# Corner and meta tiles of the first layer turned through VectorE and GpSimd's transfers instead of TensorE, the last heads' splits in another order, and one more group with widened products

## The chip, the cores and the metric

The kernel runs on one core of a Trainium2 chip. The metric is device microseconds of one execution. Three runs of the kernel before took 2268.68, 2270.69 and 2272.91 us (median 2270.69). TensorE does the matrix products, VectorE, ScalarE and GpSimd the work beside them, and the queues of SyncE, ScalarE and GpSimd issue transfers between HBM and the core's memory.

## What is computed

A decoder of two layers on 272 tokens (16 learned meta tokens ahead of 256), width 2048, 16 heads of 128. Layer 0 is attention with forget gates, layer 1 stick-breaking attention with its own keys and values; each is followed by a squared-ReLU MLP of width 8192.

```python
def forgetting_attention(q, k, v, cum_logf):
    for qs, qe in query_blocks(q.shape[1]):      # (0,16), (16,144), (144,272)
        s = jnp.einsum('bqhd,bkhd->bhqk', q[:, qs:qe], k[:, :qe]) * scale
        s = s + cum_logf[:, :, qs:qe, None] - cum_logf[:, :, None, :qe]
        s = jnp.where(mask, s, -jnp.inf)
        p = jax.nn.softmax(s, axis=-1)
        outs.append(jnp.einsum('bhqk,bkhd->bqhd', p, v[:, :qe]))
...
def squared_relu_mlp(h, w_up, w_down):
    u = h @ w_up
    return jnp.square(jax.nn.relu(u)) @ w_down
```

## The kernel before

Activations lie feature-major: 128 features on the partitions, tokens along the row. Every large product is done by `gemm_group`, one call for 512 output columns over all 2048 inputs. Weights and activations are split into a high and a low part (`whi`, `wlo` by L210 on ScalarE and L211 on VectorE; `sp.hi`, `sp.lo`), and each pair gives three products, so a call has 192 products, all issued by L177: 4 blocks `kb` of 4 chunks `kc`, 4 output tiles `m`, 3 parts. In the blocks 0 and 3 the products go output tile by output tile. The calls are counted by `u`: in layer 0 each of four **head groups** g (4 heads) has u = 3g+1 (queries), 3g+2 (keys) and 3g+3 (values); u = 61 to 64 is the output projection of layer 1, u = 89 to 92 the last quarter of its MLP's up projection, u = 93 to 95 the down projection behind it. While the split weights of one block are in use, those of the next are made; `whi`, `wlo` and the raw weights have four buffers each.

In layer 0 a product has 272 columns, from u = 61 on 256. There some products take 6 columns more (L243 to L254, `wide`): they read zeros behind the tile and write columns that nobody uses. Before the change that is done at three places of every fourth call (u % 4 == 1, output tile 3), and at three places of u = 90 (output tile 0), which follows eight products (`ph`, L785) that turn a part of the residual.

Beside the products of the next call runs the attention of a head group. In layer 0, with `s` the probabilities of 4 heads, queries on the partitions:

- `turn_probabilities` and `probabilities_back` (L446 to L459) turn the bulk of the probabilities without TensorE: VectorE turns blocks of 32 by 32 (L451), GpSimd's queue writes them to a scratch in HBM (L454, `p_dram`) and reads them back in the right order (L459). `squares`, `scratch`, `values_back` (L386 to L415) do the same for the values through `v_dram` (L394, L401, L406).
- What is left over are small pieces: the **corners** (`corners`, L434: 16 queries of the one block and 16 of the other, `sm`, or 16 values each, `vc`) and the **meta** values (`packed`, `vm`). TensorE turns them as products with a unit matrix: `pm` (L558) and `pvm` (L572, L573). ScalarE copies `pvm` into `vm_sb` (L575), VectorE makes `pm_sb` from `pm` (L560).
- `pom` (L577, L578) multiplies them, and its two halves go to the result (`put_split`) and to `own` (L581).
- `outputs` (L587), called behind the next call's 192 products, forms `po` (L596, L597) from the turned values and probabilities, adds `own` (L599), and splits the result.

Head group 3 has its values turned by TensorE (`token_major`, L374) as well, in both layers, since no call follows that would cover the transfers.

Nothing of this order on the engines is written out by hand: a scheduler with a simulated timeline places the instructions of each engine. `behind` and `placed_behind` add an order without a wait: the instruction is placed behind another, named by its place in the list `issued` of the current call's products. Each engine and each queue works off its own list in order.

Of the kernel before, what the change touches and what calls it, by code (L numbers as in the profile page):

```python
# [33 lines left out]
def yoco_kernel(ctx: ExitStack, tc: tile.TileContext, hT_in, gains, b_f, w_f, w_qkv0, w_o0, w_up, w_dn,  # L34
                w_kv, w_q1, w_o1, g_row, out):
    nc = tc.nc
# [25 lines left out]
    ident = const.tile([P, P], F32, name="ident")  # L62
# [152 lines left out]
    def gemm_group(wblk, sp, t0, evac, before={}, after={}, load_x=None):  # L215

        uid[0] += 1
        u = uid[0]  # L220
        accs = [pacc.tile([P, 512], F32, tag="acc", name=f"acc_{u}_{m}") for m in range(4)]
        n = T - t0
        for kb in range(4):
            if kb in before:
                before[kb]()
            parts, on_act, on_dve = weights(u, kb, wblk, 16 if t0 else 0, load_x)
            if kb in after:
                with tc.issue_after(on_act.ins), tc.issue_after(on_dve.ins):
                    after[kb]()

            if load_x is not None and kb == 0:
                runs = [([kc], range(4)) for kc in range(4)]
            elif kb in (0, 3):
                runs = [(range(4), [m]) for m in range(4)]
            else:
                runs = [(range(2 * hf, 2 * hf + 2), range(4)) for hf in range(2)]
            pinned[0] = load_x is None
            for kcs, ms in runs:
                pairs = ((0, sp.hi), (0, sp.lo), (1, sp.hi))
                if t0:  # L240
# [133 lines left out]
    def token_major(vT, pr, t0, label):  # L374

        pv = patt.tile([P, 2, 2, P], F32, tag="patt", name=f"pv_{label}")
        for i in range(2):
            for b in range(2):
                nc.tensor.transpose(pv[:, i, b, :], vT[:, 2 * pr + i, t0 + b * P:t0 + b * P + P], ident)
        v0 = att.tile([P, 2, 2, P], F32R, tag="v_sb", name=f"v0_{label}")  # L380
        v1 = tmp.tile([P, T], F32, tag="u2", name=f"v1_{label}")[:, :2 * P].rearrange("p (i d) -> p i d", i=2)
        split(v0, pv[:, :, 0, :])
        nc.scalar.copy(v1, pv[:, :, 1, :])
        return v0, v1

    def squares(vT, tag, label):  # L386

# [84 lines left out]
    for g in range(4):  # L472
# [74 lines left out]
        for pr in range(2):  # L547
# [10 lines left out]
        nc.tensor.transpose(pm[:, 0:P], sm, ident)  # L558
        pm_sb = att.tile([P, 192], F32, tag="pm_sb", bufs=1, name=f"pm_sb_{g}")
        nc.vector.tensor_tensor(out=pm_sb[:, :P].rearrange("p (b q) -> p b q", q=M), in1=maskD, op=ALU.mult,  # L560
                                in0=pm[:, P - M:P].unsqueeze(1).to_broadcast([P, 8, M]))

        gemm_group(w_qkv0[3 * g + 2], xa, 0, lambda m, acc: evac_kv(m, acc, vT))

# [10 lines left out]
        nc.scalar.copy(vm_sb, pv[:, :2 * P])  # L575
        po = patt.tile([P, 512], F32, tag="patt", name=f"pom_{g}")
        nc.tensor.matmul(po[:, :64], vm_sb[:, :P], s0T.rearrange("p (h q) -> p h q", h=4)[:, :, :M], start=True, stop=True)  # L577
        nc.tensor.matmul(po[:, 64:192], vm_sb[:, P:], pm_sb[:, :P], start=True, stop=True)  # L578
        put_split(ao, 4 * g, 4, 0, M, po[:, :64].rearrange("p (h q) -> p h q", h=4))
        own = att.tile([P, 8, M], F32, tag="own", bufs=1, name=f"own0_{g}")  # L580
        copied = nc.scalar.copy(own, po[:, 64:192].rearrange("p (c q) -> p c q", c=8))  # L581
        for pr in range(2):
            behind(split_probabilities(*pps[pr]), issued[-1] if pr == 0 else copied.ins)

        turned = squares(vT, "s", f"0_{g}") if g < 3 else None

        def outputs(g=g, pps=pps, vT=vT, own=own, turned=turned):  # L587
            if turned is not None:
                scratch(turned, issued[20:60:20])
                vs = values_back(turned, issued[100:120:10], issued[160:180:10], f"0_{g}")  # L590
            for pr in range(2):
                p0, p1 = in_order(*pps[pr])
                v0, v1 = vs[pr] if turned is not None else token_major(vT, pr, 0, f"0_{g}_{pr}")
# [100 lines left out]
    for g in range(4):  # L694
# [49 lines left out]
            scratch(turned, issued[-2:])  # L744

        def outputs1(g=g, vT=vT, pps=pps, pm_sb=pm_sb, turned=turned):
            for pr in range(2):
# [4 lines left out]
            nc.tensor.transpose(pv[:, :P], corners(vT[:, :, P:144], vT[:, :, 256:T], f"vc1_{g}"), ident)  # L752
            vc_sb = att.tile([P, P], F32, tag="vm_sb", bufs=1, name=f"vc_sb_{g}")
            nc.scalar.copy(vc_sb, pv[:, :P])
            own = att.tile([P, 8, M], F32, tag="own", bufs=1, name=f"own1_{g}")
            for pr in range(2):
                v0, v1 = vs[pr] if turned is not None else token_major(vT, pr, 0, f"1_{g}_{pr}")
# [152 lines left out]
```

## Time and profile before

| | |
|---|---|
| profiled execution, its own time | 2272.29 us |
| its span, first to last instruction | 2270.6 us |
| three other runs | 2268.68, 2270.69, 2272.91 us |
| TensorE busy | 2261.9 us, 18826 products |
| VectorE, ScalarE, GpSimd busy | 1345.2, 1060.1, 89.9 us |
| mean DMA rate | 190 GB/s |

Busy time says how much of the span an engine had an instruction under way; TensorE's products overlap each other, so what one costs is read from the distance between starts, not from its duration. In the rows of the timeline a row is `start, us, engine, line, operation, out<-in, xcount`, and the bracket at its end is the time that the engine sat idle before it and what ended that. Buffer numbers are left out of names.

### The profile page before, as it was taken

The page shows a single profiled execution, that of the slowest core. Times are in us where ns is not written, and L with a number is a line of the kernel's source. Part 1 is how long each engine was busy: PE and PEld are TensorE (multiplying, and loading weights), DVE is VectorE, ACT ScalarE, POOL GpSimd, SP SyncE. Part 2 cuts the span into 40 slices and gives each one's busy share as a digit, 9 for nine tenths or more (in the row PEclk, how much of TensorE's full clock was granted, in tenths as well). Part 3 has the DMA queues.
Part 4 walks back from the last instruction along what each step waited for, and adds up shares of the span by engine and source line. Part 5 has one row for each costly group of instructions (what it writes and reads, how often), then busy time and mean ns, then how long its engine had stood idle before and what let it go on. Part 6 is the DMA issues. An engine that isn't in the chain of part 4 may idle for free.

```text
span 2270.6 us, 44920 instructions
## 1 busy us (share of the span) xinstructions
PE 2261.9 (100%) x18826; PEld 2254.3 (99%) x18826; DVE 1345.2 (59%) x1947; ACT 1060.1 (47%) x1447; POOL 89.9 (4%) x178
## 2 busy tenths in 40 slices
PE   9999999999999999999999999999999999999998
PEld 9999999999999999999999999999999999999998
DVE  7767666554455455455566677666555555555555
ACT  6444445443354344344444455555444543544544
POOL 1220110000000000000000011100000000000001
PEclk9999999999999999999999999999999999999999
DMA  7765655555555555555555566665656656666564
GB/s 240 232 200 187 220 185 176 182 172 180 183 177 179 175 178 185 176 179 175 176 188 189 179 217 211 212 197 185 202 189 191 202 185 203 189 194 201 180 195 140
DMA packets 126715, 431.47 MB, mean 190 GB/s; under 512 B 15776, under 2 KB 22320, under 8 KB 126512
## 3 DMA queue, kind: packets, MB, share of 16 engines
q1 hardware_dynamic: 119520, 412.59, 56.7%
q0 software_dynamic: 4672, 12.59, 1.8%
q8 instruction: 147, 2.41, 0.4%
q10 hardware_dynamic: 2320, 3.43, 0.4%
q14 instruction: 56, 0.46, 0.1%
HBM read 416.99 MB, written 11.55 MB: 189 GB/s over the span
## 4 chain that ended last, share of the span: by engine, by line
PE 98%; DMA 1%; DVE 0%; issue 0%; ACT 0%; SPq 0%; POOL 0%; POOLq 0%; ACTq 0%
PE acc L177 96%; PE po L420 1%; PE ps L420 0%; PE pz L420 0%; DMA raw<-w_qkv 0%; PE pz L716 0%; PE ps L518 0%; DMA p_dram<-raw_p 0%; DMA raw_p<-p_dram 0%; PE po L597 0%; PE po L765 0%; DVE wlo L211 0%; ACT whi L210 0%; PE pf L339 0%; DVE raw_p L451 0%
## 5 line engine op out<-in xcount | busy, mean ns | idle before, releaser
L211 DVE TENSOR_TENSOR wlo<-raw,whi 128x1024 fp32r<-128x1024 f32 (+1 forms) x773 | 928.2, 1216 | 701.8 <-ACT whi L210 695.3
L210 ACT ACTIVATE whi<-raw 128x1024 fp32r<-128x1024 f32 (+1 forms) x773 | 797.2, 1051 | 973.8 <-PE acc L177 923.4
L177 PE MATMUL acc<-x_m,whi 128*128 128x272 f32 (+1 forms) x4096 | 644.7, 282 | 0.0
L177 PE MATMUL acc<-x_u,whi 128*128 128x272 f32 (+1 forms) x3968 | 626.1, 281 | 0.0
L177 PEld LDWEIGHTS acc<-x_m,whi 128*128 128x128 f32 x4096 | 567.3, 188 | 0.1
L177 PEld LDWEIGHTS acc<-x_u,whi 128*128 128x128 f32 x3968 | 550.3, 188 | 0.0
L177 PE MATMUL acc<-x_m,wlo 128*128 128x272 f32 (+1 forms) x2048 | 441.6, 282 | 0.0
L177 PE MATMUL acc<-x_u,wlo 128*128 128x272 f32 (+1 forms) x1984 | 431.5, 281 | 0.0
L177 PE MATMUL acc<-x_a,whi 128*128 128x272 f32 (+1 forms) x2048 | 353.3, 285 | 0.3 <-ACT whi L210 0.3
L177 PEld LDWEIGHTS acc<-x_m,wlo 128*128 128x128 f32 x2048 | 324.0, 188 | 0.0
L177 PEld LDWEIGHTS acc<-x_u,wlo 128*128 128x128 f32 x1984 | 315.1, 188 | 0.0
L177 PEld LDWEIGHTS acc<-x_a,whi 128*128 128x128 f32 x2048 | 300.7, 188 | 1.6 <-ACT whi L210 1.0
L177 PE MATMUL acc<-x_a,wlo 128*128 128x272 f32 (+1 forms) x1024 | 253.3, 285 | 0.0
L177 PE MATMUL acc<-x_kv,whi 128*128 128x272 f32 x1024 | 192.8, 288 | 0.0
L177 PEld LDWEIGHTS acc<-x_a,wlo 128*128 128x128 f32 x1024 | 175.5, 188 | 0.7 <-DVE ssq_a L143 0.4
L177 PE MATMUL acc<-x_o,whi 128*128 128x272 f32 (+1 forms) x1024 | 162.7, 282 | 0.0
L177 PEld LDWEIGHTS acc<-x_kv,whi 128*128 128x128 f32 x1024 | 160.3, 188 | 0.0
L177 PE MATMUL acc<-x_kv,wlo 128*128 128x272 f32 x512 | 147.4, 288 | 0.0
L177 PEld LDWEIGHTS acc<-x_o,whi 128*128 128x128 f32 x1024 | 141.9, 188 | 0.0
L292 DVE TENSOR_TENSOR hT<-acc,hT 128x272 f32<-128x272 f32 (+1 forms) x156 | 67.4, 432 | 75.4 <-PE acc L177 75.2
L177 PE MATMUL acc<-x_o,wlo 128*128 128x272 f32 (+1 forms) x512 | 110.5, 282 | 0.0
L177 PEld LDWEIGHTS acc<-x_kv,wlo 128*128 128x128 f32 x512 | 96.5, 188 | 0.0
(222 smaller groups left out, 1096.3 us busy)
## 6 DMA issues: line engine op xcount, KB each, us to landing
raw<-w_up SPq DMA_DIRECT2D x256, 512.0 KB, 4.3
raw<-w_dn SPq DMA_DIRECT2D x256, 512.0 KB, 4.4
raw<-w_qkv SPq DMA_DIRECT2D x92, 512.0 KB, 4.2
raw<-w_o SPq DMA_DIRECT2D x64, 512.0 KB, 4.4
raw<-w_kv SPq DMA_DIRECT2D x64, 512.0 KB, 4.5
raw<-w_q SPq DMA_DIRECT2D x32, 512.0 KB, 5.1
p_dram<-raw_p POOLq DMA_DIRECT2D x32, 96.0 KB, 3.7
raw_p<-p_dram POOLq DMA_DIRECT2D x8, 384.0 KB, 5.5
```

The costliest lines, as they stand in the source:

```text
L177: ins = nc.tensor.matmul(*args, **kw).ins
L210: on_act = nc.scalar.activation(hp, src, AF.Copy)
L211: on_dve = nc.vector.tensor_tensor(out=lp, in0=src, in1=hp.bitcast(F32), op=ALU.subtract)
L292: nc.vector.tensor_tensor(out=hT[:, c, t0:], in0=acc, in1=hT[:, c, t0:], op=ALU.add)
L420: product = nc.tensor.matmul(out, a[i], b[j], start=start and k == 0, stop=stop and k == 2)
```

## The change

Three parts, each in words and then in the diff.

**Corners and meta tiles of layer 0.** `corner_turned` (new) turns the corner `sm` on VectorE, 32 partitions by 128, and sends it through a scratch `c_dram` on GpSimd's queue, one write and one read; the result is `pmq`, and VectorE makes `pm_sb` from it. `rows_turned` (new) does so for `vm` and `vc` in head groups 0 to 2: two turns on VectorE, four writes to `m_dram` and one read into `vm_sb`. The products `pm` (all four head groups) and `pvm` (groups 0 to 2) and the copy into `vm_sb` (0 to 2) are gone; `pom` moves from the middle of the next call into `outputs`, behind it. The split of the second pair's probabilities moves there too.

**Head group 3 of layer 1.** `outputs1` asks for the turned values (`token_major`) ahead of the split of the second pair's probabilities.

**Widened products.** u = 91 gets the same three places as u = 89 and u = 93.

```diff
-                wide = [(0, 0, 0), (1, 0, 1), (2, 1, 1)] if t0 and u % 4 == 1 else []
+                wide = [(0, 0, 0), (1, 0, 1), (2, 1, 1)] if t0 and (u % 4 == 1 or u == 91) else []
...
+    c_dram = tc.dram_tile([4, 32, M], F32, name="c_dram")
+    m_dram = tc.dram_tile([2, 4, 32, 4, 32], F32, name="m_dram")
...
+    def corner_turned(sm, label):
+
+        r = att.tile([P, P], F32, tag="pk", name=f"pkT_{label}")
+        nc.vector.transpose(r[P - 32:], sm[P - 32:])
+        q = att.tile([P, M], F32, tag="pmq", bufs=1, name=f"pmq_{label}")
+        nc.gpsimd.dma_start(c_dram.rearrange("b i q -> i b q"), r[P - 32:].rearrange("i (b q) -> i b q", b=4)[:, :, 32 - M:])
+        nc.gpsimd.dma_start(q, c_dram.rearrange("b i q -> (b i) q"))
+        return q
+
+    def rows_turned(packs, dst, write, read, label):
+
+        n = len(packs)
+        t = att.tile([P, 2 * P], F32, tag="vt", bufs=1, name=f"vt_{label}")[:, :n * P]
+        for k, src in enumerate(packs):
+            nc.vector.transpose(t[:, k * P:k * P + P], src)
+        for a in range(4):
+            behind(nc.gpsimd.dma_start(m_dram[:n].rearrange("k c j a x -> a j (k c) x")[a],
+                                       t[32 * a:32 * a + 32].rearrange("j (m x) -> j m x", x=32)), write)
+        behind(nc.gpsimd.dma_start(dst.rearrange("p (k y) -> p k y", k=n), m_dram[:n].rearrange("k c j a x -> (c j) k (a x)")), read)
...
-        pm = patt.tile([P, 512], F32, tag="patt", name=f"pm_{g}")
-        sm = corners(s[:, :, P:144], s[:, :, 400:416], f"sm_{g}")
-        nc.tensor.transpose(pm[:, 0:P], sm, ident)
...
+        pmq = corner_turned(corners(s[:, :, P:144], s[:, :, 400:416], f"sm_{g}"), f"0_{g}")
...
-        pv = patt.tile([P, 512], F32, tag="patt", name=f"pvm_{g}")
         vm = packed(vT[:, :, 0:32], f"vm_{g}")
-        product = nc.tensor.transpose(pv[:, P:2 * P], corners(vT[:, :, P:144], vT[:, :, 256:T], f"vc_{g}"), ident)
-        placed_behind(nc.tensor.transpose(pv[:, :P], vm, ident), product)
+        vc = corners(vT[:, :, P:144], vT[:, :, 256:T], f"vc_{g}")
...
+        behind(split_probabilities(*pps[0]), issued[-1])
         turned = squares(vT, "s", f"0_{g}") if g < 3 else None
...
             if turned is not None:
+                behind(split_probabilities(*pps[1]), issued[60])
                 scratch(turned, issued[20:60:20])
                 vs = values_back(turned, issued[100:120:10], issued[160:180:10], f"0_{g}")
+                rows_turned([vm, vc], vm_sb, issued[112], issued[130], f"0_{g}")
+                small_outputs()
...
         def outputs1(g=g, vT=vT, pps=pps, pm_sb=pm_sb, turned=turned):
-            for pr in range(2):
-                behind(split_probabilities(*pps[pr]), issued[((36, 72) if g < 3 else (20, 40))[pr]])
             if turned is not None:
+                for pr in range(2):
+                    behind(split_probabilities(*pps[pr]), issued[(36, 72)[pr]])
                 vs = values_back(turned, issued[64:80:8], issued[112:128:8], f"1_{g}")
+            else:
+                behind(split_probabilities(*pps[0]), issued[20])
+                vs = [token_major(vT, pr, 0, f"1_{g}_{pr}") for pr in range(2)]
+                behind(split_probabilities(*pps[1]), vs[1][2])
```

`small_outputs` holds the former lines L576 to L581, the products `pom` and what reads them.

How the scheduler places this. **TensorE, end of u = 4 (queries of head group 1), where `outputs` of head group 0 stands.** Before, the last products of u = 4, then all of `po`, then the first products of u = 5 (`acc_0_1518`):

```order
L177 MATMUL acc_3_1226<-x_a_139,wlo_3_1_1416 128x272
L420 MATMUL po_0_0_1491<-p_0_0_910,v_0_0_0_1481 128x256 x3
L597 MATMUL po_0_0_1491<-raw_p_0_0_909,v_0_0_0_1482 128x128
L420 MATMUL po_0_0_1491<-p_0_0_910,v_0_0_0_1481 128x256 x3
L597 MATMUL po_0_0_1491<-raw_p_0_0_909,v_0_0_0_1482 128x128
L420 MATMUL po_0_1_1503<-p_0_1_922,v_0_0_1_1486 128x256 x3
```

With the change, inside u = 5 (its output tile 2, of which 9 products stand ahead; 12 each of the tiles 0 and 1 stand before those):

```order
L177 MATMUL acc_2_1529<-x_a_139,whi_0_1_1539 128x272 x2
L177 MATMUL acc_2_1529<-x_a_139,wlo_0_1_1540 128x272
L598 MATMUL pom_1494<-s0T_909,vm_sb_1200 128x64
L599 MATMUL pom_1494<-pm_sb_943,vm_sb_1200 128x128
L421 MATMUL po_0_0_1500<-p_0_0_912,v_0_0_0_1476 128x256 x3
L623 MATMUL po_0_0_1500<-raw_p_0_0_911,v_0_0_0_1477 128x128
```

`pom` and `po` of head group 0 have moved 33 products into u = 5. In the head groups 1 and 2 `pom` stands right behind the 192nd product of the call, directly ahead of `po`.

**GpSimd's queue for head group 0**, from the read of the first probabilities to the end of the values' way. Before:

```order
L459 DMA raw_p_0_0_909<-p_dram_145 128x768
L401 DMA v_dram_147<-turned_0_1211 32x4x128 x4
L431 COPY pk_vm_1191<-vT_0_152 128x128
L438 COPY pk_vc_1193<-vT_0_152 128x4x16 x2
L459 DMA raw_p_0_1_921<-p_dram_146 128x768
L401 DMA v_dram_148<-turned_0_1211 32x4x128 x4
L406 DMA turned_0_1211<-v_dram_147 128x512
L406 DMA turned_0_1211<-v_dram_148 128x512
```

With the change:

```order
L480 DMA raw_p_0_0_911<-p_dram_145 128x768
L447 DMA c_dram<-pkT_0_938 32x4x16
L402 DMA v_dram_149<-turned_0_1204 32x4x128 x4
L432 COPY pk_vm_1195<-vT_0_154 128x128
L480 DMA raw_p_0_1_923<-p_dram_146 128x768
L402 DMA v_dram_150<-turned_0_1204 32x4x128 x4
L448 DMA pmq_0_940<-c_dram 128x16
L439 COPY pk_vc_1197<-vT_0_154 128x4x16 x2
L407 DMA turned_0_1204<-v_dram_149 128x512
L458 DMA m_dram<-vt_0_1486 32x8x32 x4
L407 DMA turned_0_1204<-v_dram_150 128x512
L460 DMA vm_sb_1200<-m_dram 128x2x128
```

Seven transfers are new (L447, L448, four of L458, L460); the second read of the values stands behind the writes to `m_dram`. On VectorE the turn of `vc` (L456) stands behind `wlo_3_1` of u = 4.

**ScalarE in u = 61**, where head group 3 of layer 1 is finished. Before:

```order
L370 ACTIVATE p_3_0_16768<-raw_p_3_0_16760 128x512
L370 ACTIVATE p_3_1_16800<-raw_p_3_1_16792 128x512
L210 ACTIVATE whi_2_0_17258<-raw_2_0_17254 128x2x512
L210 ACTIVATE whi_2_1_17262<-raw_2_1_17255 128x2x512
L754 COPY vc_sb_17145<-pvc_17140 128x128
L370 ACTIVATE v_1_3_0_17153<-pv_3_0_17148 128x256
L210 ACTIVATE whi_3_0_17318<-raw_3_0_17314 128x2x512
```

With the change:

```order
L372 ACTIVATE p_3_0_16794<-raw_p_3_0_16786 128x512
L210 ACTIVATE whi_2_0_17284<-raw_2_0_17280 128x2x512
L210 ACTIVATE whi_2_1_17288<-raw_2_1_17281 128x2x512
L372 ACTIVATE v_1_3_0_17169<-pv_3_0_17164 128x256
L372 ACTIVATE v_1_3_1_17179<-pv_3_1_17174 128x256
L784 COPY vc_sb_17191<-pvc_17186 128x128
L210 ACTIVATE whi_3_0_17344<-raw_3_0_17340 128x2x512
L385 COPY v_1_3_0_17170<-pv_3_0_17164 128x256
L385 COPY v_1_3_1_17180<-pv_3_1_17174 128x256
L372 ACTIVATE p_3_1_16826<-raw_p_3_1_16818 128x512
```

The split of the second pair's probabilities (`p_3_1`) has moved from ahead of the weights of block 2 to behind those of block 3 and the value copies. On TensorE the turns of both pairs' values (`pv_3_0`, `pv_3_1`) now stand together behind block 0 of u = 61, and the first two products of `po` stand behind 26 products of block 1, where 32 stood before.

More of the change, by code (lines that the diff above doesn't have):

```diff
@@ L382, in token_major @@
         split(v0, pv[:, :, 0, :])
-        nc.scalar.copy(v1, pv[:, :, 1, :])
-        return v0, v1
+        return v0, v1, nc.scalar.copy(v1, pv[:, :, 1, :]).ins
     def squares(vT, tag, label):
@@ L553, in yoco_kernel @@
             pps.append((raw, p0))
-        pm = patt.tile([P, 512], F32, tag="patt", name=f"pm_{g}")
-        sm = corners(s[:, :, P:144], s[:, :, 400:416], f"sm_{g}")
[L558 to L561, printed above, removed]
+        pmq = corner_turned(corners(s[:, :, P:144], s[:, :, 400:416], f"sm_{g}"), f"0_{g}")
@@ L563, in yoco_kernel @@
+        pm_sb = att.tile([P, P], F32, tag="pm_sb", bufs=1, name=f"pm_sb_{g}")
+        nc.vector.tensor_tensor(out=pm_sb.rearrange("p (b q) -> p b q", q=M), in1=maskD, op=ALU.mult,
+                                in0=pmq.unsqueeze(1).to_broadcast([P, 8, M]))
         gemm_group(w_qkv0[3 * g + 2], xa, 0, lambda m, acc: evac_kv(m, acc, vT))
         probabilities_back(pps, (140, 176 if g else 191), nc.gpsimd)
-        pv = patt.tile([P, 512], F32, tag="patt", name=f"pvm_{g}")
         vm = packed(vT[:, :, 0:32], f"vm_{g}")
-        product = nc.tensor.transpose(pv[:, P:2 * P], corners(vT[:, :, P:144], vT[:, :, 256:T], f"vc_{g}"), ident)
@@ L573, in yoco_kernel @@
-        placed_behind(nc.tensor.transpose(pv[:, :P], vm, ident), product)
+        vc = corners(vT[:, :, P:144], vT[:, :, 256:T], f"vc_{g}")
         vm_sb = att.tile([P, 2 * P], F32, tag="vm_sb", bufs=1, name=f"vm_sb_{g}")
[L575 to L578, printed above, removed]
@@ L579, in yoco_kernel, with small_outputs @@
-        put_split(ao, 4 * g, 4, 0, M, po[:, :64].rearrange("p (h q) -> p h q", h=4))
         own = att.tile([P, 8, M], F32, tag="own", bufs=1, name=f"own0_{g}")
-        copied = nc.scalar.copy(own, po[:, 64:192].rearrange("p (c q) -> p c q", c=8))
-        for pr in range(2):
-            behind(split_probabilities(*pps[pr]), issued[-1] if pr == 0 else copied.ins)
+        behind(split_probabilities(*pps[0]), issued[-1])
         turned = squares(vT, "s", f"0_{g}") if g < 3 else None
-        def outputs(g=g, pps=pps, vT=vT, own=own, turned=turned):
+        def small_outputs(g=g, vm_sb=vm_sb, pm_sb=pm_sb, s0T=s0T, own=own):
+            po = patt.tile([P, 512], F32, tag="patt", name=f"pom_{g}")
+            nc.tensor.matmul(po[:, :64], vm_sb[:, :P], s0T.rearrange("p (h q) -> p h q", h=4)[:, :, :M], start=True, stop=True)
+            nc.tensor.matmul(po[:, 64:192], vm_sb[:, P:], pm_sb, start=True, stop=True)
+            put_split(ao, 4 * g, 4, 0, M, po[:, :64].rearrange("p (h q) -> p h q", h=4))
+            return nc.scalar.copy(own, po[:, 64:192].rearrange("p (c q) -> p c q", c=8))
@@ L588, in outputs @@
+        if turned is None:
+            pv = patt.tile([P, 512], F32, tag="patt", name=f"pvm_{g}")
+            product = nc.tensor.transpose(pv[:, P:2 * P], vc, ident)
+            placed_behind(nc.tensor.transpose(pv[:, :P], vm, ident), product)
+            nc.scalar.copy(vm_sb, pv[:, :2 * P])
+            behind(split_probabilities(*pps[1]), small_outputs().ins)
+        def outputs(g=g, pps=pps, vT=vT, own=own, turned=turned, vm=vm, vc=vc, vm_sb=vm_sb, small_outputs=small_outputs):
             if turned is not None:
+                behind(split_probabilities(*pps[1]), issued[60])
@@ L589, in outputs @@
                 scratch(turned, issued[20:60:20])
                 vs = values_back(turned, issued[100:120:10], issued[160:180:10], f"0_{g}")
+                rows_turned([vm, vc], vm_sb, issued[112], issued[130], f"0_{g}")
+                small_outputs()
             for pr in range(2):
                 p0, p1 = in_order(*pps[pr])
-                v0, v1 = vs[pr] if turned is not None else token_major(vT, pr, 0, f"0_{g}_{pr}")
+                v0, v1 = vs[pr] if turned is not None else token_major(vT, pr, 0, f"0_{g}_{pr}")[:2]
@@ L756, in outputs1 @@
             for pr in range(2):
-                v0, v1 = vs[pr] if turned is not None else token_major(vT, pr, 0, f"1_{g}_{pr}")
+                v0, v1 = vs[pr][:2]
                 po = patt.tile([P, 2, 256], F32, tag="patt", name=f"po1_{g}_{pr}")
```

1 line of the change is left out of this document (removed).

## The prediction

> **What bounds the kernel now.** I read the page's busy times and its chain first, then TensorE's waits, then single rows of the timeline where the change cuts.
>
> ```profile
> span 2270.6 us, 44920 instructions
> ...
> PE 2261.9 (100%) x18826; PEld 2254.3 (99%) x18826; DVE 1345.2 (59%) x1947; ACT 1060.1 (47%) x1447; POOL 89.9 (4%) x178
> ...
> PE 98%; DMA 1%; DVE 0%; issue 0%; ACT 0%; SPq 0%; POOL 0%; POOLq 0%; ACTq 0%
> ```
>
> TensorE is busy from one end to the other and makes 98% of the chain that ended last. So time goes away only where TensorE has fewer products, a shorter wait, or a quicker pace. The view of who waited for whom has four rows for TensorE, together 3.0 us; this one lies in the change's reach:
>
> ```profile
> PE po L420 <- ACT v L370: 0.8, 1, 0.8
> ```
>
> **Term A, the turns that leave TensorE.** The chain gives the pace of 272 columns, the timeline (rows of start and duration) the place of one `pm` and of one `pvm` pair:
>
> ```profile
> 111.22 23.69 PE acc L177 x192
> ...
> 82.04 0.29 PE L177 MATMUL acc<-x_a,whi 128*128 128x272 f32 x1
> 82.17 0.27 PE L558 MATMUL pm<-ident,pk_sm 128*128 128x128 f32 x1
> 82.19 0.37 PE L177 MATMUL acc<-x_a,whi 128*128 128x272 f32 x1
> 82.40 0.29 PE L177 MATMUL acc<-x_a,wlo 128*128 128x272 f32 x1
> ...
> 93.26 0.29 PE L177 MATMUL acc<-x_a,whi 128*128 128x272 f32 x1
> ...
> 93.52 0.37 PE L177 MATMUL acc<-x_a,whi 128*128 128x272 f32 x1
> 93.73 0.28 PE L177 MATMUL acc<-x_a,wlo 128*128 128x272 f32 x1
> ```
>
> 23.69 / 192 = 0.1234 us per product. From 82.04 to 82.40 two products start and one turn lies between: 0.36 - 0.247 = 0.11 us for the turn (its 0.27 of duration overlaps its neighbours). From 93.26 to 93.73 with two turns: 0.47 - 0.247 = 0.22. Gone are four `pm` (4 x 0.115 = 0.46) and three `pvm` pairs (3 x 0.22 = 0.67): **-1.13 us**. `pom` stays, at another place and the same price.
>
> The Trainium skill speaks against this edit: "VectorE: DVE Perf Modes", Rules for kernel authors, wants a 128x128 transpose on TensorE where PSUM will do. By that rule A would be left undone, 1.13 us of no gain. The rows above show why it does not decide here: the turn is cheap, but on the only engine that is never idle.
>
> **What takes their place** is VectorE's and GpSimd's. A turn of 128x128 on VectorE is this group's:
>
> ```profile
> L394 DVE STREAM_TRANSPOSE turned<-vT x48: 267/276/314, 81.2 to 1417.0; 128x128 f32<-128x128 f32 x48
> ```
>
> Per head group that is two such turns and one of 32 partitions (between nothing and the same 0.28): at most 0.84 us of VectorE, and one copy less for ScalarE. VectorE is 59% busy, and where it sits idle in this stretch it waits for the weights that ScalarE splits (the bracket in the next rows); I cost it at nothing. Were that cover gone, it would be the 0.84 per head group. The wait that the change adds is TensorE's at `pom`, for `vm_sb` out of `m_dram`: behind it in TensorE's list stand `po` and all that follows. The worst place is head group 0:
>
> ```profile
> 97.61 1.23 DVE L211 TENSOR_TENSOR wlo<-raw,whi 128x1024 fp32r<-128x1024 f32 x1 [1.95 <-ACT whi L210]
> ...
> 88.00 1.65 POOL L401 DMA_DIRECT2D v_dram<-turned  x3 [0.18 <-issue]
> ...
> DMA to landing us min/median/max: 2.0/4.4/7.0
> ...
> turned<-v_dram POOLq DMA_DIRECT2D x12, 256.0 KB, 5.7
> ...
> 97.06 0.33 PE L577 MATMUL pom<-s0T,vm_sb 128*128 128x64 f32 x2
> ...
> 97.64 0.41 PE L177 MATMUL acc<-x_a,whi 128*128 128x272 f32 x2
> ...
> 108.90 0.36 PE po L420 x3
> ```
>
> The turn of `vc` stands behind `wlo_3_1`, the row at 97.61. With the 0.34 us that head group 0 has lost on TensorE by then, it ends at 98.8. An issue on GpSimd's queue takes 0.55 (1.65 for three), so the last of the four writes starts at 100.5 and lands, by the median of 4.4, at 104.9; the read of `vm_sb` lands 5.7 later, at 110.6. TensorE came to `po` at 108.90. Now it comes 0.34 earlier, a further 0.46 earlier for the `pom` that left (97.06 to 97.64, less one product), and 33 products (4.07) later: 112.2. So 1.6 us are to spare at medians. With the slowest landing twice (7.0) the read lands at 114.5 and TensorE waits 2.3. The writes have 256 pieces of 128 bytes where a write to `v_dram` has 128 of 512, which no row shows; if each of the five issues took twice as long, 2.8 us more, the median would make 113.4 and a wait of 1.2. Ends: 0 and 5.1 (both); I take **+0.3**, nearer the median chain, since it is built on rows of the same queue. For the head groups 1 and 2 the same sum has room:
>
> ```profile
> 166.27 0.57 POOL L406 DMA_DIRECT2D turned<-v_dram  x1 [0.19 <-issue]
> ...
> 185.81 0.36 PE po L420 x3
> ```
>
> The writes start at 166.8, the last lands at 172.9, `vm_sb` at 178.6; TensorE comes at 185.81 less 1.1, so 6.1 us are to spare. The second read of the values in head group 0 is pushed behind the writes to 101.1 and lands at 106.8; its split stands in ScalarE's list behind that of the queries, which needs the last product of u = 4, and `po` of the second pair comes 33 products later. `pmq` is wanted only by the same `pom` and comes far sooner.
>
> **Term B, head group 3 of layer 1.** Rows of TensorE, ScalarE and SyncE's queue in u = 61:
>
> ```profile
> 1473.01 0.27 PE L752 MATMUL pvc<-ident,pk_vc 128*128 128x128 f32 x1
> ...
> 1476.31 1.07 PE L177 MATMUL acc<-x_o,whi 128*128 128x256 f32 x8
> 1478.19 0.51 PE L420 MATMUL po<-p,v 128*128 128x256 f32 x2 [0.81 <-ACT v L370]
> ...
> 1475.18 0.63 ACT L370 ACTIVATE p<-raw_p 128x512 fp32r<-128x512 f32 x1 [5.83 <-DMA raw_p<-p_dram]
> 1475.71 1.99 ACT L210 ACTIVATE whi<-raw 128x1024 fp32r<-128x1024 f32 x2
> ...
> 1477.76 0.39 ACT L370 ACTIVATE v<-pv 128x256 fp32r<-128x256 f32 x1
> ...
> 1471.88 18.79 SPq L199 DMA_DIRECT2D raw<-w_o  x8
> ...
> raw<-w_o SPq DMA_DIRECT2D x64, 512.0 KB, 4.4
> ```
>
> ScalarE stood 5.83 us at the second pair's probabilities, made the weights of block 2 and only then the values that `po` wanted. Eight products from 1476.31 at 0.1133 (below) end at 1477.22; `po` started at 1478.19: 0.97 us. With the change the weights of block 2 are asked for as soon as block 0 is done (about 1473) and take 1.99, so the values are split by 1475.4. TensorE comes to `po` after four turns more and six products less, at about 1477.0. The wait goes: **-0.97**. What is late next is `p_3_1`, behind the weights of block 3: those land 4.4 after their issue at 1471.88, at 1476.3; then 1.0 for one of them, two copies of 0.4 (as the split of the values) and the 0.6 of `p_3_1` itself make 1478.7, and VectorE's half about 1479.4. Between the first `po` and that of the second pair stand 18 products of the call (2.0) and nine others of at least 0.11, so TensorE asks for it at 1480.0 or later. No new wait.
>
> **Term C, the pace of the 256-column products.** Three stretches of 22 us (TensorE's products in brackets, then the clock), and rows of starts:
>
> ```profile
> 2082.00:2104.00 22.00, 22.00 (x197) 1.00 0.59 190
> 2128.00:2150.00 22.00, 22.00 (x189) 1.00 0.60 191
> ...
> 2178.00:2200.00 22.00, 22.00 (x197) 1.00 0.60 188
> ...
> 2103.97 1.04 PE L785 MATMUL ph<-ident,hT 128*128 128x128 f32 x8
> 2104.76 1.19 PE L177 MATMUL acc<-x_m,whi 128*128 128x262 f32 x8
> ...
> 2131.72 1.10 PE L177 MATMUL acc<-x_m,whi 128*128 128x256 f32 x8
> ...
> 2176.94 1.09 PE L177 MATMUL acc<-x_u,whi 128*128 128x262 f32 x8
> ...
> 2195.56 0.62 PE L177 MATMUL acc<-x_u,wlo 128*128 128x256 f32 x4
> ...
> 2196.92 0.62 PE L177 MATMUL acc<-x_u,wlo 128*128 128x256 f32 x4
> ```
>
> All are the same products at clock 1.00, yet the middle stretch holds 189 and the others 197. Twelve products from 2195.56 to 2196.92 take 0.1133 each; the 384 from 2131.72 to 2176.94 take 0.1178. The slow pace begins behind the turns `ph` at 2103.97, and the wide products of u = 90, which stand right there, did not end it. It ended where the first wide product of u = 93 stands, 2176.94. The change puts one at the same place of u = 91, which is the row at 2131.72. If it works as in u = 93: 384 x (0.1178 - 0.1133) = **-1.71**, less at most 0.02 for three products of 6 more columns (6/256 of 0.1133 each by size, a few times that with what follows them).
>
> The Trainium skill, "TensorE: Matmul & The Clock Gate", Back-to-back issue gap, gives a width one gap whatever came before it (N/2.4 + 2.5 ns: 109 ns for 256 columns, an estimate by that page). By it C would be nothing and the wide products a pure cost. The two counts above speak against it.
>
> **The sum.** -1.13 + 0.3 - 0.97 - 1.69 = -3.5. Against the profiled execution, 2272.29, that is 2268.8. The median of the runs shown, 2270.69, is 1.6 below it, and the sum from there gives 2267.2; whether those runs had the slow stretch I can't see. I take the middle, 2268.0.
>
> **The rivals.**
>
> 1. *The slow pace outlives u = 91.* One wide product was seen to end it, three were seen not to. Then C is gone: 2269.7.
> 2. *TensorE waits at `pom` of head group 0.* For it: that read is the last thing that GpSimd's queue brings, and pieces of 128 bytes are not in the trace. Against: 1.6 us to spare at medians. A wait between 1.2 and 3.5, and nothing else amiss: about 2270.
> 3. *The last heads' wait stays under another name* (a split on ScalarE or VectorE that comes later than worked out), the edit not doing what it is there for: 2269.0.
> 4. *Slower: the small pieces make the scratch's way longer in all three head groups.* If writes and read together take x us more than the medians, TensorE waits x - 1.6 in head group 0 and x - 6.1 in each of 1 and 2. From x = 5.4 the gains of 3.8 are gone; at x = 7.4 it is 8.4 us of waits, and 2276. Against: the rearranged writes to `v_dram` of 512-byte pieces land within 7.0 at the slowest. The Trainium skill has this as a rule ("DMA: Bandwidth & Descriptors", Rules for kernel authors: a transpose by a plain DMA with a rearranged access pattern costs 19 times the hardware one); the landings above, on just such writes, do not bear it out, and here VectorE has turned the blocks already.
> 5. *More than the sum:* no wait in head group 0, and runs as quick as the median shown: 2266.5.
>
> **How the numbers follow.** Chances: forecast 0.40, rival 1 0.22, 2 0.15, 3 0.08, 4 0.06, 5 0.09. The predicted time is the forecast's, 2268.0. The range goes from 2265.7, below rival 5, to 2271.3, above rivals 1 to 3 and the common wait of rival 2; it leaves out rival 4 and tails. A measurement of this kernel can tell about 0.2% from no change, which is 4.5 us: faster by more means below 2266.1. That takes rival 5 in part and the forecast's quick tail, 0.18; slower by more, above 2275.2, is the far half of rival 4, 0.04; within 0.2% is 0.78.
>
> **What would show it.** A: no rows `pm` and `pvm` in head groups 0 to 2. In head group 0 the row of `pom` has no idle bracket that names `vm_sb<-m_dram`; a bracket of some microseconds there is rival 2, and in three head groups rival 4. B: `po` at about 1475 without the 0.81. C: 196 or 197 products in 22 us from some 4 us into u = 91 on; 189 there is rival 1. If the stretch behind `ph` runs at 197 already in u = 90, C was chance and the prediction's largest term is wrong.

## The result, and the profile after

The changed kernel takes **2267.62 us** (median of 22 runs, 2266.57 to 2269.02); the kernel before, run beside it, 2271.23 (22 runs, 2268.68 to 2275.09). The ratio is 0.9985, with a 95% interval of 0.9979 to 0.9991: 3.6 us less, within the 0.2% that the prediction called no change, and 0.4 us from its number (2268.0). The spread of the runs fell from 6.4 us to 2.5. How much of this is what the prediction said it was is another question, and the experiments answer it differently from the sum.

The page of the changed kernel (profiled execution 2266.66 us):

```profile
span 2264.9 us, 44932 instructions
...
PE 2257.3 (100%) x18816; PEld 2249.7 (99%) x18816; DVE 1347.1 (59%) x1957; ACT 1059.2 (47%) x1444; POOL 105.2 (5%) x201
...
PE 99%; DMA 0%; ACT 0%; DVE 0%; issue 0%; POOL 0%; POOLq 0%; SPq 0%; ACTq 0%; DVEq 0%
```

TensorE has ten instructions fewer (18826 to 18816: four `pm`, six `pvm`). GpSimd has 15.3 us more (issues of DMAs), VectorE 1.9. TensorE's waits, all four rows of the view:

```profile
PE idle L61 <- DVE mean_w L57: 1.1, 1, 1.1
PE pr_fin L177 <- DVE fin L852: 0.8, 1, 0.8
PE acc L177 <- ACT x_a L125: 0.3, 1, 0.3
PE acc L177 <- DVE wlo L211: 0.2, 1, 0.2
```

The row of `po` behind ScalarE's `v` is gone, and none names `vm_sb<-m_dram`. The timeline has the two places of which the prediction spoke, `pom` of head group 0 and `po` in u = 61 (start, duration; the bracket is the idle time before):

```profile
99.04 1.79 POOL L458 DMA_DIRECT2D m_dram<-vt  x3 [6.55 <-DVE pm_sb L579]
103.38 0.60 POOL L458 DMA_DIRECT2D m_dram<-vt  x1 [2.55 <-issue]
...
108.30 0.72 POOL L460 DMA_DIRECT2D vm_sb<-m_dram  x1 [3.76 <-DMA m_dram<-vt]
...
111.90 0.33 PE L598 MATMUL pom<-s0T,vm_sb 128*128 128x64 f32 x2
...
1473.15 0.64 ACT L372 ACTIVATE v<-pv 128x256 fp32r<-128x256 f32 x2
...
1476.38 0.65 ACT L372 ACTIVATE p<-raw_p 128x512 fp32r<-128x512 f32 x1
...
1475.63 0.40 PE L421 MATMUL po<-p,v 128*128 128x256 f32 x2
```

`pom` has no bracket. ScalarE makes the values (1473.15) ahead of the second pair's probabilities (1476.38), and `po` does not wait. And the pace behind `ph`, stretches of 22 us with TensorE's instructions in brackets:

```profile
2082.00:2104.00 22.00, 22.00 (x196) 1.00 0.62 192
2106.00:2128.00 22.00, 22.00 (x196) 1.00 0.56 179
2128.00:2150.00 22.00, 22.00 (x196) 1.00 0.62 196
2178.00:2200.00 22.00, 22.00 (x196) 1.00 0.59 196
```

The slow stretch is not there. But it is not there in the second stretch either, which ends before the new wide products of u = 91 stand. By the prediction's own last test, that makes C a gain that this execution did not need.

**Where TensorE's time differs.** I counted the `acc` products (18,336 in every trace) and took the time between the starts of the same two products in each profiled execution. Between the 12,001st and the 16,801st it is 544.57 us in every trace with wide products before `ph`, to the hundredth. So a difference is not spread over the kernel; it sits in named places. The first column is the start of the 193rd product; the second the time from there to the 9,001st (layer 0's heads and most of its MLP); the third from the 11,401st to the 11,701st (the end of u = 60 and most of u = 61); the fourth from the 16,801st to the 18,301st (around `ph`); the last from there to the end of the span.

| execution | start | 193 to 9001 | u = 61 | around `ph` | end |
|---|---|---|---|---|---|
| before | 32.43 | 1112.88 | 40.10 | 181.08 | 18.17 |
| before, second profile (e12) | 32.96 | 1112.88 | 39.47 | 178.36 | 18.17 |
| A alone (e1) | 33.57 | 1111.92 | 39.01 | 178.36 | 17.68 |
| B alone (e2) | 32.29 | 1112.88 | 38.99 | 178.37 | 18.16 |
| C alone (e3) | 33.08 | 1112.88 | 39.02 | 178.38 | 18.17 |
| A and B (e4) | 34.03 | 1111.68 | 38.98 | 178.37 | 17.73 |
| changed | 32.32 | 1111.68 | 38.98 | 178.39 | 17.68 |
| changed, again (e5) | 32.55 | 1111.76 | 38.98 | 178.39 | 17.68 |

The profiled pair differs by 5.6 us: 0.1 in the start, 1.2 in A's stretch, 1.1 in u = 61, 2.7 around `ph`, 0.5 at the end.

### The profile page after: what moved, and what is told of

Read it like the earlier page. It is cut to its first block, busy times and chain, and to the rows that moved or that the text cites. A ratio compares the mean times of both kernels' runs of the same rounds, so it can differ in the third digit from the quotient of the medians.

```text
span 2264.9 us, 44932 instructions
## 1 busy us (share of the span) xinstructions
PE 2257.3 (100%) x18816; PEld 2249.7 (99%) x18816; DVE 1347.1 (59%) x1957; ACT 1059.2 (47%) x1444; POOL 105.2 (5%) x201
## 4 chain that ended last, share of the span: by engine, by line
PE 99%; DMA 0%; ACT 0%; DVE 0%; issue 0%; POOL 0%; POOLq 0%; SPq 0%; ACTq 0%; DVEq 0%
PE acc L177 97%; PE po L421 1%; PE ps L421 0%; PE pz L421 0%; DMA raw<-w_qkv 0%; PE pz L742 0%; PE ps L539 0%; PE po L623 0%; PE po L795 0%; DMA hT<-hT_in 0%; ACT whi L210 0%; PE pf L341 0%; DVE wlo L211 0%; PE pv L381 0%; ACT x_a L125 0%
```

## The experiments

**Each part alone, and the change without C.** e1 is the kernel before with the transfers and what they need, e2 with the new order in `outputs1`, e3 with the one line on u = 91; e4 is the changed kernel with that line put back. Of e1, e2 and e4:

```
-        nc.tensor.transpose(pm[:, 0:P], sm, ident)
+        pmq = corner_turned(corners(s[:, :, P:144], s[:, :, 400:416], f"sm_{g}"), f"0_{g}")
...
+                rows_turned([vm, vc], vm_sb, issued[112], issued[130], f"0_{g}")
+                small_outputs()
```

```
+                behind(split_probabilities(*pps[0]), issued[20])
+                vs = [token_major(vT, pr, 0, f"1_{g}_{pr}") for pr in range(2)]
+                behind(split_probabilities(*pps[1]), vs[1][2])
```

```
-                wide = [(0, 0, 0), (1, 0, 1), (2, 1, 1)] if t0 and (u % 4 == 1 or u == 91) else []
+                wide = [(0, 0, 0), (1, 0, 1), (2, 1, 1)] if t0 and u % 4 == 1 else []
```

> The kernel before with the transfers in place of the corner and meta turns alone (all four corner tiles, the meta and corner values of head groups 0 to 2). Theory (three separate gains): 0.9 to 1.1 us less than the kernel before, no wait at pom, and the stretch behind ph still at 189 products in 22 us in some executions. Rival (the pace is all): the same time as the kernel before within 0.5 us. Rival (the phase of the work upstream sets the pace behind ph): 3 us or more less, with 197 products per 22 us from u = 90 on.

> The kernel before with the last heads' split order alone. Theory: 0.8 to 1.0 us less than the kernel before, no wait at po in u = 61. Rival (the wait goes but the time is lost behind it): within 0.3 us of the kernel before. Rival (phase sets the pace): 3 us or more less, 197 products per 22 us from u = 90 on.

> The kernel before with the wide products of u = 91 alone. Theory of the prediction: 1.7 us less, the slow pace ends at the first wide product of u = 91 where it appears, and the spread of the runs is narrower. Rival (the slow stretch comes by chance and u = 91 does nothing to it): the same median and the same spread as the kernel before, 189 products per 22 us still seen behind u = 91 when the profile has it.

> The changed kernel without the wide products of u = 91. Theory of the prediction: 2.0 us less than the kernel before (1.1 and 0.9), 1.7 more than the changed kernel, and a slow stretch from ph to u = 93. Rival (phase: the work upstream is what keeps the pace fast): the time of the changed kernel, 3.6 less than before, with 197 products per 22 us in u = 90. Rival (chance): a median between the two with the wide spread of the kernel before, 6 us.

Measured beside the kernel before at 2269.59 (33 runs, 2268.4 to 2273.45): A alone 2267.82, ratio 0.9991 (0.9982 to 1.0); B alone 2268.48, 0.9993 (0.9984 to 1.0002); C alone 2269.48, 1.0 (0.9991 to 1.0009); A and B 2267.33, 0.9989 (0.998 to 0.9998). **C alone is worth 0.1 us in the median, and A with B are worth 2.3.** An interval is some 2 us to each side, so the parts are told apart by the table, not by these ratios. There a steady 1.7 for C falls: around `ph` e3 takes 178.38 and e2, without C, 178.37.

The table shows A in 193 to 9001: 1112.88 without it, 1111.68 with it where `pom` did not wait, **1.20 us**. In e1 it is 1111.92: TensorE reached `pom` 0.24 us too early, where no wait was expected. And the span ends 0.49 us sooner behind the 18,301st product (0.44 in e4) in these executions with A's transfers, a gain that the prediction has no term for. It lies in the last write of `out`: ScalarE's queue issues it 6.18 us behind the start of the last `acc` product in the kernel before and in the changed one, and it lands 2.83 us later in the one and 2.34 in the other. Why it lands sooner is not shown.

For B, u = 61 takes 38.98 or 38.99 in each execution with the new order, but with the old order 40.10, 39.47, 39.01 and 39.02. **The wait was there in two executions of four.** These are the rows of the old order, ScalarE's second pair and TensorE's `po`, first of e1:

```profile
1474.02 0.63 ACT L372 ACTIVATE p<-raw_p 128x512 fp32r<-128x512 f32 x1 [4.23 <-DMA raw_p<-p_dram]
...
1477.67 0.40 PE L421 MATMUL po<-p,v 128*128 128x256 f32 x2
```

of e3:

```profile
1474.40 0.63 ACT L370 ACTIVATE p<-raw_p 128x512 fp32r<-128x512 f32 x1 [4.41 <-DMA raw_p<-p_dram]
...
1477.87 0.40 PE L420 MATMUL po<-p,v 128*128 128x256 f32 x2
```

and of e12, the second profile of the kernel before:

```profile
1475.08 0.63 ACT L370 ACTIVATE p<-raw_p 128x512 fp32r<-128x512 f32 x1 [5.20 <-DMA raw_p<-p_dram]
...
1478.09 0.51 PE L420 MATMUL po<-p,v 128*128 128x256 f32 x2 [0.19 <-ACT v L370]
```

In the two executions that waited, `po` starts 3.01 us behind ScalarE's start on the second pair (1475.18 and 1478.19 in the first profile, 1475.08 and 1478.09 here). In the two that did not, 3.01 later would have been 1477.03 and 1477.41, and TensorE came at 1477.67 and 1477.87, with 0.64 and 0.46 to spare. So what B saves depends on when the read of `p_dram` lands against TensorE, and that differs by more than a microsecond from one execution to the next.

**Once more, and without wide products behind `ph`.** e5 is the changed kernel itself; e6 takes the wide products of u = 90 (these lines) and of u = 91 away, e7 those of u = 90 alone, e8 all (it has `wide = []` in place of these lines):

```
-                if u == 90:
-                    wide = [(0, 0, 0), (0, 0, 1), (0, 2, 1)]
```

> The changed kernel once more, on this chip beside the next three and the kernel before. Theory, as the first four experiments left it (A is 1.1 us less work on TensorE in every execution; B and C only take away what comes in some executions, a late transfer at u = 61 and a slow stretch behind ph): 2267.3, as without the wide products of u = 91, and 2 to 2.5 us less than the kernel before. Rival (C is a steady gain of 1.7): 3.6 less than the kernel before and 1.7 less than the run without the wide products.

> The changed kernel without the wide products of u = 90 and of u = 91; those of every fourth call stay. Theory (the turns ph leave TensorE in the slow pace, the wide products of u = 90 end it in most executions): 189 products per 22 us from ph to the first wide product of u = 93, some 640 products of 0.0045 us, so 2.9 us more than the changed kernel. Rival (the pace behind ph is chance, the wide products have no part): 196 or 197 per 22 us and the time of the changed kernel.

> The changed kernel without the wide products of u = 90 but with those of u = 91. Theory (a wide product ends the slow pace wherever it stands): slow from ph to the first wide product of u = 91, some 240 products, 1.1 us more than the changed kernel, and 196 or 197 per 22 us behind it. Rival 1 of the prediction (u = 91 does not end it): slow to u = 93, 2.9 us more. Rival (chance): no difference.

> The changed kernel without any wide product. Theory (short turns leave the slow pace behind and nothing else ends it): the 256-column calls of layer 1 from the outputs of the heads on at 189 products per 22 us, u = 62 to 95 less than 6500 products of 0.0045 us, up to 29 us more. By the page of the Trainium skill weighed in the prediction (one gap per width): no difference. Rival (the slow pace ends by itself at the next evacuation or call): under 3 us more.

Measured beside the kernel before at 2269.94 (33 runs): e5 2267.60, 0.9988 (0.9979 to 0.9996), so 2.3 less, and C adds nothing to e4's 2.3 here either. e6 2270.12, 0.9999 (0.999 to 1.0008), 2.5 over e5. e7 2268.29, 0.9991 (0.9982 to 1.0), 0.7 over e5. e8 2272.44, 1.001 (1.0001 to 1.0019), 4.8 over e5. The stretches of e6:

```profile
2082.00:2104.00 22.00, 22.00 (x196) 1.00 0.62 192
2106.00:2128.00 22.00, 22.00 (x189) 1.00 0.59 189
2128.00:2150.00 22.00, 22.00 (x189) 1.00 0.59 191
2178.00:2200.00 22.00, 22.00 (x196) 1.00 0.59 192
```

of e7, whose first wide product behind `ph` stands at 2130.00:

```profile
2106.00:2128.00 22.00, 22.00 (x189) 1.00 0.58 182
2128.00:2150.00 22.00, 22.00 (x196) 1.00 0.62 192
2178.00:2200.00 22.00, 22.00 (x197) 1.00 0.61 194
```

and of e8:

```profile
2082.00:2104.00 22.00, 22.00 (x197) 1.00 0.62 192
2106.00:2128.00 22.00, 22.00 (x189) 1.00 0.59 191
2128.00:2150.00 22.00, 22.00 (x190) 1.00 0.58 191
2178.00:2200.00 22.00, 22.00 (x189) 1.00 0.60 186
```

**This shows what starts and ends the slow pace here.** Without wide products right behind `ph` it begins there in all three, at a clock of 1.00. It ends where the first wide product stands: at u = 93 in e6, at u = 91 in e7, nowhere in e8. Between the 16,801st and 18,301st products e6 takes 181.07 and e7 179.38, so u = 91's wide products took **1.69** off, where C's working had 1.71. But with those of u = 90 in place (every other profile: before, changed, e1 to e5, e9 to e12) the slow pace came in one execution of eleven, the first one that I read. The expectation of up to 29 us for e8 was wrong: ahead of `ph` its pace is the quick one (197 from 2082), so in these executions only the turns `ph` started the slow pace, and the wide products of the earlier calls had nothing to end. Eight turns in a row are not enough for it: in u = 61 e8 has as many, `pv`, also among products of 256 columns and without a wide one, and what follows is quick.

```profile
1473.36 1.03 PE L379 MATMUL pv<-ident,vT 128*128 128x128 f32 x8
...
1484.00:1506.00 22.00, 22.00 (x196) 1.00 0.56 171
```

What sets `ph` apart from `pv` is not shown.

e6 also shows rival 2. Its 193 to 9001 takes 1112.79, 1.11 over the rest:

```profile
PE pom L595 <- DMA vm_sb<-m_dram: 0.8, 1, 0.8
```

**A late read, more room for the scratch, a second profile.** In e9 (on the kernel before) and e10 (on the changed one) the last head group reads its second pair's probabilities twice from the same place:

```
         probabilities_back(pps, (140, 184), nc.sync)
+        if g == 3:
+            probabilities_back(pps[1:], (184,), nc.sync, 1)
```

e11 is the changed kernel with GpSimd's copy of the corner values ahead of the second half of the values' writes, and the rows' own writes and read asked for earlier:

```
+                if copy is not None and pr == 1:
+                    behind(ins, copy)
...
-                rows_turned([vm, vc], vm_sb, issued[112], issued[130], f"0_{g}")
+                rows_turned([vm, vc], vm_sb, issued[70], issued[108], f"0_{g}")
```

> The kernel before with the second pair's probabilities of the last head group of layer 1 read twice out of the scratch (the same data), so that they come some 3 us later in every execution. Theory (what the last heads' order saves is set by when that read lands; in the rows so far po starts 3.1 us after the landing at the earliest, with 0.5 us to spare in two executions and 1.0 missing in one): a wait of 2 to 3.5 us at po in u = 61 and 2 to 3 us more than the kernel before. Rival (the order of ScalarE, not the read, made the wait): within 0.5 us of the kernel before. Beside that: if a wait at u = 61 is what brings the slow stretch behind ph, 189 products per 22 us behind ph.

> The changed kernel with the same second read. Theory (the values no longer stand behind these probabilities on ScalarE, and the probabilities are wanted only by the second pair, about 3 us later): no wait at the first po, a wait of at most 0.5 us at the second pair, the time within 0.5 us of the changed kernel (2267.6), so 4 to 5 us less than the kernel before with the same second read. Rival (the wait only moves to the second pair's po): 2 us or more over the changed kernel.

> The changed kernel with the copy of the corner values on GpSimd ahead of the second half of the values' writes, and the writes and the read of the scratch for the meta and corner rows asked for earlier. Theory (the spare time at pom of head group 0 is what is left of the scratch's way): the turn of the corner values ends one weight split earlier, about 2.9 us, vm_sb lands 2 to 4 us before pom (1.07 in the changed kernel's profile), and the time is that of the changed kernel less 0.2 (the mean of the waits seen at pom), inside the uncertainty. Rival (the queue is full anyway, the fourth write waits for the first to land): vm_sb lands as late as before.

> The kernel before once more, one look. Theory (wait at po and slow stretch come in some executions only): a span between 2266 and 2271 that is the sum of the start, a wait of 0 to 1.1 at po in u = 61 and 0 or 2.7 behind ph. Rival (both are steady in the kernel before): 1.0 at po and 189 products per 22 us behind ph, as in the first profile.

Measured beside the kernel before at 2269.34 (27 runs): e9 2270.79, 1.0005 (0.9996 to 1.0014); e10 2267.60, 0.9988 (0.9979 to 0.9998); e11 2267.19, 0.9987 (0.9978 to 0.9996); e12, one run, 2269.45.

e9 was expected at 2 to 3 us more and a wait at the first `po`; it came 1.5 more, with the wait elsewhere:

```profile
1475.85 0.39 ACT L370 ACTIVATE v<-pv 128x256 fp32r<-128x256 f32 x1
1480.14 0.63 ACT L370 ACTIVATE p<-raw_p 128x512 fp32r<-128x512 f32 x1 [3.90 <-DMA raw_p<-p_dram]
...
1478.44 0.40 PE L420 MATMUL po<-p,v 128*128 128x256 f32 x2
...
1482.03 0.49 PE L767 MATMUL po<-raw_p,v 128*128 128x128 f32 x2 [1.22 <-ACT v L383]
```

The added read also moved the split in ScalarE's list: `p` (1480.14) now stands behind the high half of the first pair's values (1475.85) and ahead of the low half, for which TensorE waits at 1482.03. So e9 does not repeat the old order with a later read, and its number is no price of that. In its profile u = 61 takes 40.51, 1.5 over the old order without a wait; the span also ends 0.36 later (18.53 against 18.17). What it does show is that a stall of ScalarE at this read can cost TensorE when values stand behind it (in e1 and e3 stalls of 4.2 and 4.4 us cost nothing). e10 has no values behind it. Its ScalarE stands at the same read too, and TensorE's waits are only the two at the kernel's ends:

```profile
1477.23 0.63 ACT L372 ACTIVATE p<-raw_p 128x512 fp32r<-128x512 f32 x1 [1.12 <-DMA raw_p<-p_dram]
...
1475.46 0.40 PE L421 MATMUL po<-p,v 128*128 128x256 f32 x2
...
1478.83 0.36 PE L421 MATMUL po<-p,v 128*128 128x256 f32 x1
```

e10's time is that of e5, as expected. The 4 to 5 us expected between e9 and e10 are 3.2, because e9 lost less than expected. The added read has a price at the end of the span in both: the span ends 1.34 us behind the last landing of `out`, against 0.91 without it.

In e9 and in e12, which both waited in u = 61, the pace behind `ph` is the quick one, so such a wait does not bring the slow stretch.

e11's `vm_sb` gained less than the 2 to 4 us expected:

```profile
96.88 1.77 POOL L462 DMA_DIRECT2D m_dram<-vt  x3 [3.79 <-DVE pm_sb L583]
102.07 0.60 POOL L462 DMA_DIRECT2D m_dram<-vt  x1 [3.42 <-issue]
...
106.94 0.72 POOL L464 DMA_DIRECT2D vm_sb<-m_dram  x1 [3.71 <-DMA m_dram<-vt]
...
112.69 0.33 PE L603 MATMUL pom<-s0T,vm_sb 128*128 128x64 f32 x2
```

The writes start 2.2 us sooner, and 3.0 sooner if counted from the 193rd product (33.12 here, 32.32 in the changed kernel), which is the 2.9 expected. But the fourth again stands still until the first has landed, and the read takes 4.40 us, where it took 2.53. So it landed 1.35 us before `pom`, against 1.07 in the changed kernel, and `pom` did not wait. The median is the lowest of all, but against the runs beside it e11 is 2.2 less, where e5 was 2.3 less: no difference, and no version here beats the changed kernel.

**A stretch outside the table.** From the 9,001st to the 11,401st product (the end of layer 0 and most of layer 1's heads) ten executions take 307.30 to 307.32 us. The other four, all with A's transfers, take 307.59 (e1), 307.60 (e4), 308.32 (e8) and 309.14 (e11). There `po` of an earlier head group of layer 1 waits for its values; these are the rows of e8 and of e11:

```profile
PE po L419 <- ACT v L370: 0.5, 1, 0.5
```

```profile
PE po L423 <- DVE v L373: 0.8, 1, 0.8
```

Five other executions with A and all five without it have no such wait. No run shows whether A has a part in it.

## Why the prediction came out, and which of its terms did not

**The number held because terms that were too large met one that was missing and an execution that had everything.** So the mechanisms were right, but the nearness of the sum is in part luck. By steps:

1. *TensorE is the only engine that counts.* Right: outside of the table's stretches and of the waits in layer 1's heads, executions of the same pace agree to hundredths of a microsecond.
2. *Term A, -1.13.* Right: -1.20, in every execution. VectorE's and GpSimd's share of it cost nothing in that stretch but the wait of the next step; whether the waits in layer 1's heads (0.3 to 1.8 us in four of nine executions with A) have to do with it stays open.
3. *The scratch wait at `pom`, +0.3.* Right in size. The eight executions with this scratch order (changed, e1, e4 to e8, e10) waited 0, 0.24, 0, 0.08, 1.11, 0, 0.08 and 0: 0.19 on average. Two steps of its working were wrong and cancelled: I let the four writes follow each other at 0.55, so that the last would start at 100.5 and land at 104.9; it started at 103.38 and landed at 107.90. And I let the read take 5.7, the figure of 256 KB; it took 2.5 for 128 KB (2.4 to 3.3 in these eight). What was left to spare was 1.07 in the first profile and nothing in e1, not 1.6. The issues did not take twice as long: 0.60 for one against 0.55.
4. *Rival 4, three waits.* Fell: head groups 1 and 2 did not wait in any execution.
5. *Term B, -0.97.* The mechanism was right: the row is gone, `po` came at 1475.63, and e10 shows that the probabilities behind it have room. The size was that of one execution. Over the four with the old order u = 61 took 39.40 on average, against 38.98 with the new one: **-0.4**. The step that failed is "the wait goes: -0.97", a single row taken for a steady cost. The prediction also put `p_3_1` at 1478.7 and its need at 1480.0; they were 1477.0 and 1479.0. By then TensorE stood 1.3 earlier than in the profile that the sum was read from (1.2 by A, 0.1 by the start), so both were close.
6. *Term C, -1.69.* The mechanism was right to the hundredth (e6 and e7: 1.69), and rival 1 fell. The page of the Trainium skill weighed against it ("TensorE: Matmul & The Clock Gate", Back-to-back issue gap, one gap per width) does not hold for this stream: e8 has the same 256 columns at 189 or at 197 per 22 us, by what stood before them. The section gives that gap for a product by itself, and says that in a stream of weight loads and products both set the spacing. But that the wide products of u = 90 did not end it was read from the one execution of eleven in which they failed. There C is worth 1.7; in the others the table shows nothing for it. **This is the mis-sized term**: some 1.7 / 11, so 0.15 on average.
7. *Missing:* the 0.49 us at the end of the span. It comes in the executions with A (0.40 to 0.50), and e10 ends 0.42 sooner than e9, which has the same added read without A.

The terms as measured make -1.20 + 0.19 - 0.42 - 0.15 - 0.49 = -2.1, beside 2.3 measured in e4 and in e5. The 3.6 of the result itself is larger, and its interval (2.0 to 4.8) holds both. In that comparison 11 of 22 runs of the kernel before were over 2271, against 4 of 33, 7 of 33 and 6 of 27 in the later ones; its profiled execution had both the late read and the slow stretch, 3.8 us together. If about half of those runs had the slow stretch, as that one did, C's share would be some 0.85 there (half of 1.7), and some 0.8 of the 3.6 would still have no name. No run shows that, since a run without a profile gives no more than its time; why the wide products of u = 90 fail in some executions, and whether that comes more often on one chip than on another, stays open. So does why the last write of `out` lands sooner, which gives the 0.49.

## What to carry to other kernels

A wait or a slow stretch that one profile shows is an event until a second profile of the same kernel shows it: count instructions from a fixed one, lay two executions side by side, and price as steady only what stands in both. In a kernel that one engine fills, such a table finds tenths of a microsecond that medians with intervals of 2 us cannot. An edit that takes away a rare event should move the spread more than the median. The spread fell from 6.4 to 2.5 us here, but e4, without C, has one of 2.0 over 11 runs, so which part did it is not shown.

## What the runs showed of the hardware

- **One width, two lasting paces.** Products of 256 columns run at 0.1133 or 0.1178 us for hundreds in a row at a granted clock of 1.00; the eight turns `ph` start the slow pace (e6, e7, e8), one product of 262 columns ends it (e6, e7), and in e8, which has none, it lasted for more than 100 us. In one execution of eleven, the first profile of the kernel before, three such products right behind `ph` did not end it, and in e8 the eight turns `pv` of u = 61 did not start it.
- **GpSimd's queue holds a write back until an earlier one has landed.** The fourth write to `m_dram` was issued 0.32 or 0.33 us after the first had landed in each of the nine executions with these writes (103.38 after 103.06 in the changed kernel, 102.07 after 101.74 in e11). A write has 256 pieces, so three of them hold 768, and 1024 with the fourth. In head group 1 of the changed kernel the second, third and fourth write are issued at 168.99, 170.30 and 171.10, each 0.32 or 0.33 us after a landing (168.67, 169.98, 170.77). With 128 pieces for each write to `v_dram` and for its read, the pieces under way and those of the next write come to 1024 ahead of each of these landings and to 896, 896 and 768 behind it. So the queue seems to take a write only while that sum is under 1024; no run was made to test it.
- **The start differs most.** The 193rd product started between 32.15 and 34.03 us over all the profiles, with no order by kernel: a spread of 1.9 us. The 22 runs of the changed kernel spread by 2.5.
